# A gated-recurrence and linear-attention layer: column sums in another bank, sample gates in one accumulator, first values by halves

## The chip, the cores and the metric

The kernel runs on one core of one Trainium2 chip. Its time is the device time of that core in microseconds (us). Before the change it is 1463.81 us, the median of three runs (1462.57 to 1464.4). The core has five engines that run side by side, each through its own list of instructions in order: TensorE (PE) multiplies matrices, VectorE (DVE) and ScalarE (ACT) work on rows of elements, GpSimd (POOL) does some more of that, and SyncE (SP) mostly issues transfers (DMA). They wait for one another by semaphores.

## The reference

One layer works on a prompt of 2048 tokens and on 8 single-token samples, with a model width of 1024. Cut to what matters here:

```python
hn = _rmsnorm(x, g_norm) * (1.0 + scale[:, None]) + shift[:, None]
z = hn @ w_in
xa, za, q, k, v, glr, zg = jnp.split(z, SPLITS, axis=-1)
xc = conv_b + sum(xp[:, j:j + T] * conv_w[j] for j in range(CONV_W))
xb = xc.reshape(Bn, T, LRU_BLOCKS, LRU_BW)
gx = jax.nn.sigmoid(jnp.einsum('btnd,nde->btne', xb, w_gate_x).reshape(Bn, T, D_LRU) + b_gate_x)
ga = jax.nn.sigmoid(jnp.einsum('btnd,nde->btne', xb, w_gate_a).reshape(Bn, T, D_LRU) + b_gate_a)
log_a = (LRU_C * ga.astype(f32)) * jax.nn.log_sigmoid(lru_lambda.astype(f32))
a = jnp.exp(log_a)
u = jnp.sqrt(-jnp.expm1(2.0 * log_a)) * (gx * xc).astype(f32)
_, h = lax.associative_scan(_lin_comb, (a, u), axis=1)
y_lru = h.astype(x.dtype) * jax.nn.silu(za)
...
y_gla = o.reshape(Bn, T, D_GLA).astype(x.dtype) * jax.nn.silu(zg)
mix = jnp.concatenate([y_lru, y_gla], axis=-1) @ w_out
x = x + gate[:, None] * mix
```

Left out is the attention that makes o from q, k, v and the decay of glr. Both the prompt and the samples go through the layer, and the states (the last h, the last conv rows, the attention state) are outputs too.

## The kernel before

Products are made exact enough in float32 by splitting each operand into a high and a low part and adding three products (high by high, low by high, high by low): such triples are the lines L396 to L398, L1571, L1703 to L1706 and L1775 to L1777.

The prompt is worked in two halves of 1024 tokens. In the first half the columns of the input projection that are not attention come in **couples** (about 328 to 598 us): eight `Lru` couples (a block of 128 columns of xa and the same block of za) and three `Zg` couples (gate columns of the attention), in the order Lru 0 to 2, Zg(0, 3), Lru 3 to 7, Zg(0, 0), Zg(0, 1). Then come the attention heads, and in the second half (880 to 1115 us) eight Lru couples and three Zg couples again, then the output projection.

A couple computes a product of two 128-column blocks and two 512-token segments by seven products of 12 matmuls (`product`, q = 0 to 6, L1571), a scheme that saves an eighth of the matmuls by adding and subtracting operands first. Products 0 and 3 go to an accumulator x, 1, 4 and 6 to y, 2 and 5 to a third, zz. x and zz are PSUM banks of the tag `acc`, which has four of them; y is one of two `tp` banks. A third pair of banks, of the tags `kv` and `o`, is handed out in turn by `gps()` (L1473).

In an Lru couple the products' results go to ACT and DVE as they end. After product 3 and product 5 the convolution of a segment (`conv`: ACT L1682, L1683, DVE L1685 three times) gives `cv`; it is split into `xh` (ACT L1690) and `xl` (DVE L1691). The **gates** of a segment are then six matmuls into two `gps` banks (L1703, L1704, L1706), each read by an ACT tanh (L1707, into `tx` and `tg`). After the second segment follow on ACT exp (L1716), square root (L1717) and a table change (L1718, `one`), on DVE two products (L1724, L1725), the scan (L1731), and the multiplication of its result with the silu of za (`zs`, ACT L1135; DVE L1740), which is then stored to `mixd`. In a Zg couple the silu is multiplied with blocks of the attention output, which are loaded ahead (`load_o`); of the four blocks the third goes to the place `am`, the fourth to `xh` or `t2`.

For the samples, `combine` in the first half has PE form the column sums of the raw weights (`sample_cols`: eight matmuls L304 into a bank taken from `acc`, a copy to SBUF by ACT, L305, and after a delay of 1.25 units two small matmuls L310 into the same bank, which DVE L312 reads). The copy's place is `am`, a tile that else holds gate weights; in the first couple and in those that follow a Zg, whose third block of the attention output lies in `am`, it is a tile of the tag `xa`, the convolution's input. In the second half, `sample_gates` follows each Lru couple's second gates: three matmuls of 8 columns into a `gps` bank and a tanh, for each of two gates (L1775 to L1777, L1778).

`values` is the projection of one attention head's values: eight tiles of 128 tokens, each 24 matmuls over k = 0 to 7 (L396 to L398) into an `acc` bank; for the second half's first head it stands right behind the last couple. Its weights come in two transfers, k = 0 to 3 and k = 4 to 7 (SP, from `parts`).

The order of the work is that in which the code calls for it; pieces handed to `after(units, f)` are called when so many units have passed, and `behind(engine)` puts an instruction after the engine's last. A couple's `wait` (0.75) delays `combine`. The column sums of a couple are made two couples ahead of its own products. Within that, a scheduler settles the order of each engine.

Of the kernel before, what the change touches and what calls it, by code (L numbers as in the profile page):

```python
# [8 lines left out]
F32 = mybir.dt.float32  # L9
# [5 lines left out]
P = 128  # L15
D = 1024
KT = D // P
T = 2048
TH = T // 2
NS = 8  # L20
# [33 lines left out]
def hybrid_kernel(ctx, tc, i, o):  # L54
# [7 lines left out]
    def acc():  # L62
        return psum.tile([P, 512], F32, tag="acc", name="acc", bufs=4)
# [65 lines left out]
    hbx = cp.tile([P, KT], F32, name="hbx")  # L129
    hba = cp.tile([P, KT], F32, name="hba")  # L130
# [159 lines left out]
    zsam = cp.tile([P, 24, NS], F32, name="zsam")  # L290
# [102 lines left out]
    def value_mm(ps, c, w, n, kts):  # L393
        for kt in range(*kts):
            hi, lo, _ = w[kt // 4]
            PE.matmul(ps, part(0, kt, c), hi[:, kt % 4], start=kt == 0, stop=False)  # L396
            PE.matmul(ps, part(0, kt, c), lo[:, kt % 4], start=False, stop=False)  # L397
            PE.matmul(ps, part(1, kt, c), hi[:, kt % 4], start=False, stop=kt == KT - 1)  # L398
# [9 lines left out]
    begun = {}  # L408
# [501 lines left out]
    def values(half, h, w):  # L910
        first = h == HEADS[0]
        n = DV + (RANK if first else 0)
        vh, vl = new_values()
        turns = []
        for tt in range(8):
            c = slice(tt * P, (tt + 1) * P)
            ps = acc()
            value_mm(ps[:, :n], c, w, n, (0, KT))
            hi, lo = vh[tt // 4][:, tt % 4], vl[tt // 4][:, tt % 4]
            S.copy(hi, ps[:, :DV])  # L920
            V.tensor_tensor(lo, ps[:, :DV], hi.bitcast(F32), op=OP.subtract)
            if tt == 0 and half == 1 and first:
                raws = [raw_rows(V0 + h * DV, n, k0, 4) for k0 in (0, 4)]
            elif tt == 0:
                raws = [x[2] for x in w]
            if tt == 3 * half + 1 and own_samples(half, h):
                after(0.5, sample_values(h, raws, n))
            if len(turns) == 3 or tt == 7 and turns:
                turns.pop(0)()
            if first:  # L930
                turns.append(low_rank(ps[:, DV:n], slice(0, P), tt * P))
            tick(0.5)
        for f in turns:
            after(1, f, True)
        return vh, vl
# [535 lines left out]
    banks, turns = [0], [0, 0, 0, 1]  # L1471

    def gps():  # L1473
        banks[0] ^= 1
        return psum.tile([P, 512], F32, tag=("kv", "o")[banks[0]], name="gps", bufs=1)

    class Couple:
# [63 lines left out]
        def combine(self, q=G):  # L1541
            r = self.raw
            b11, b12, b21, b22 = [r[:, 4 * k:4 * k + 4, b] for k in range(2) for b in range(2)]
            if self.half == 0:
                tmp = am.rearrange("p c t -> p (c t)")
                if self.own_tmp:
                    tmp = lp.tile([P, 512 + 4], F32, tag="xa", name="tmp")
                sample_cols(lambda kt: r[:, kt].rearrange("p b n -> p (b n)"), 2 * P,
                            [(zsam[:, n], 1.0) for n in self.sam], tmp, acc, 1.25)
            t = self.t2 = lp.tile([P, 4, P], F32, tag="t2", name="t2")  # L1550
            q.tensor_tensor(b11, b12, b11, op=OP.subtract)
            q.tensor_tensor(t, b22, b11, op=OP.subtract)
            q.tensor_tensor(b12, b22, b12, op=OP.subtract)

        keep, wait, more, own_tmp = None, 0.75, (), False

        def begin(self):
            pass
# [42 lines left out]
    class Zg(Couple):  # L1601
# [8 lines left out]
                self.src = wtd[n]  # L1610

        def product(self, q):
            for n in {1: (0, 1), 2: (2,), 5: (3,)}.get(q, ()):
                if n == 3:
                    x = (lp.tile([P, 512], F32, tag="t2", name="o4") if self.turn == 1 else
                         lp.tile([P, 512], F32R, tag="xh", name="o4").bitcast(F32))
                elif n == 2 and self.turn == 1:
                    x = lp.tile([P, 512], F32R, tag="xl", name="o").bitcast(F32)
                else:
                    x = o_places[n]  # L1620
                self.o.append(x)
                self.load_o(n)
            super().product(q)
# [146 lines left out]

    def sample_gates(t):
        x, j = smp_lru, t.j
        for g, bias in enumerate((hbx, hba)):
            ps = gps()[:, :NS]
            PE.matmul(ps, t.wgh[:, g], x["h"][:, j], start=True, stop=False)  # L1775
            PE.matmul(ps, t.wgh[:, g], x["l"][:, j], start=False, stop=False)
            PE.matmul(ps, t.wgl[:, g], x["h"][:, j], start=False, stop=True)  # L1777
            S.activation((zsam[:, 16:24], x["t"])[g][:, j], ps, AF.Tanh, bias=bias[:, j:j + 1], scale=0.5)  # L1778
        x["n"] += 1
        if x["n"] == KT:  # L1780
            after(2, samples_lru)
# [58 lines left out]
    def couples(cs, lead=5, at={}):  # L1840

        n = len(cs)
        for k in (1, 2):
            cs[-k].turn = k
        for c, prev in zip(cs[1:], cs):
            c.own_tmp = isinstance(prev, Zg)
        cs[0].own_tmp = True
        uses = [(0, 0), (0, 1)]
        for m in range(n):
# [44 lines left out]
    w = None  # L1894
# [529 lines left out]
    for n in range(2, 16):  # L2424
        g = n - 1
# [88 lines left out]
```

## Time and profile before

| | us |
|---|---|
| median of 3 runs | 1463.81 |
| profiled execution | 1455.25 |
| its span | 1453.5 |
| PE busy | 1408.9 |
| DVE busy | 1063.0 |
| ACT busy | 726.3 |
| POOL busy | 206.7 |
| span of the first half's couples, about | 270 |
| span of the second half's couples, about | 235 |

One execution is profiled; its own time is 1455.25 us, below the median of the others. The views that the prediction quotes are the page (busy time of each engine), windows (busy time of PE, its weight loads PEld, DVE, ACT and POOL in a stretch, then the granted TensorE clock as a share of full speed, the DMA share and GB/s), the list of waits (which instruction stood still, behind which, total us, how often, longest), and the timeline (start, duration, engine, line, operation, output and inputs, count; in brackets the idle time before it and what ended it). A row of the timeline with x12 is twelve like instructions in a run.

### The profile page before, as it was taken

How to read it: one execution, taken by the hardware profiler on the slowest of the kernel's cores; microseconds unless marked ns; L12 is line 12 of the kernel's file. 1: busy time of each engine (PE TensorE's matmuls, PEld its weight loads, DVE VectorE, ACT ScalarE, POOL GpSimd, SP SyncE). 2: the span in 40 equal slices, each digit the busy share in tenths (PEclk: the TensorE clock that was granted, in tenths of full speed). 3: DMA queues.
4: the chain of work that ended last, by engine and by line, in shares of the span. 5: the costliest groups of instructions: out<-in, count | busy, mean ns of one | idle time of the engine just before them, and what ended most of it. 6: DMA issues, size and time to landing. Idle time of an engine off the chain costs nothing.

```text
span 1453.5 us, 22471 instructions
## 1 busy us (share of the span) xinstructions
PE 1408.9 (97%) x8113; PEld 1167.0 (80%) x8113; DVE 1063.0 (73%) x2357; ACT 726.3 (50%) x1343; POOL 206.7 (14%) x257
## 2 busy tenths in 40 slices
PE   7999999999999999899999999999999999999997
PEld 5888989886868777789898888787788787777886
DVE  5767976657869786666777864787855886588886
ACT  4634463635775877333343433767663622244332
POOL 0200154325223222001211100000012000000000
PEclk9999999999999999999999999999999999999999
DMA  9724666648678567964957528898879767684452
GB/s 327 268 87 157 255 218 216 236 139 299 248 243 288 178 228 254 341 222 150 342 176 242 188 100 308 277 303 284 275 239 384 310 242 263 235 331 145 143 168 102
DMA packets 173380, 341.89 MB, mean 235 GB/s; under 512 B 12466, under 2 KB 101842, under 8 KB 169677
## 3 DMA queue, kind: packets, MB, share of 16 engines
q1 hardware_dynamic: 136981, 275.82, 55.4%
q0 software_dynamic: 13680, 48.64, 8.7%
q10 hardware_dynamic: 22608, 15.99, 3.5%
q8 instruction: 64, 1.05, 0.3%
q14 instruction: 47, 0.39, 0.1%
HBM read 205.78 MB, written 134.69 MB: 234 GB/s over the span
## 4 chain that ended last, share of the span: by engine, by line
PE 65%; DVE 14%; DMA 7%; ACT 6%; issue 5%; POOL 2%; SPq 0%; ACTq 0%; POOLq 0%; DVEq 0%
PE acc L2161 11%; PE tp L2161 8%; PE acc L1571 8%; PE tp L1571 7%; PE acc L397 4%; PE acc L396 4%; PE acc L398 4%; PE acc L702 3%; PE acc L704 3%; PE acc L703 3%; DVE cv L1685 2%; PE po L1059 2%; DVE a L1731 1%; DVE op L1518 1%; DMA scratch<-in_x_prompt_dram 1%
## 5 line engine op out<-in xcount | busy, mean ns | idle before, releaser
L1571 PE MATMUL acc<-op,op 128*128 128x512 f32 x1056 | 257.3, 395 | 3.7 <-ACT zs L1135 3.7
L1571 PEld LDWEIGHTS acc<-op,op 128*128 128x128 f32 x1056 | 199.2, 190 | 48.4 <-ACT zs L1135 5.4
L1571 PE MATMUL tp<-op,op 128*128 128x512 f32 x792 | 195.2, 394 | 3.2 <-DVE acc L1581 1.8
L2161 PE MATMUL acc<-w,a 128*128 128x512 f32 (+1 forms) x792 | 187.7, 389 | 2.5 <-DVE w L2026 2.0
L2161 PEld LDWEIGHTS acc<-w,a 128*128 128x128 f32 x792 | 146.6, 188 | 39.1 <-issue 3.4
L1571 PEld LDWEIGHTS tp<-op,op 128*128 128x128 f32 x792 | 146.4, 188 | 38.5 <-issue 2.9
L396 PE MATMUL acc<-w,op 128*128 128x256 f32 (+1 forms) x508 | 150.8, 297 | 3.3 <-DMA w<-parts 2.0
L397 PE MATMUL acc<-w,op 128*128 128x256 f32 (+1 forms) x508 | 144.8, 285 | 0.4 <-DVE w L375 0.4
L398 PE MATMUL acc<-w,op 128*128 128x256 f32 (+1 forms) x508 | 144.9, 285 | 0.2 <-DVE op L271 0.2
L2161 PE MATMUL tp<-w,a 128*128 128x512 f32 x564 | 137.3, 393 | 0.0
L2161 PEld LDWEIGHTS tp<-w,a 128*128 128x128 f32 x564 | 105.1, 188 | 28.3 <-issue 5.2
L702 PE MATMUL acc<-op,w 128*128 128x512 f32 x296 | 121.1, 409 | 0.0
L704 PE MATMUL acc<-op,w 128*128 128x512 f32 x296 | 116.5, 394 | 0.0
L703 PE MATMUL acc<-op,w 128*128 128x512 f32 x296 | 115.9, 392 | 0.0
L396 PEld LDWEIGHTS acc<-w,op 128*128 128x128 f32 x508 | 97.0, 191 | 5.5 <-ACT op L1321 2.6
L397 PEld LDWEIGHTS acc<-w,op 128*128 128x128 f32 x508 | 96.3, 190 | 1.5 <-DVE w L375 0.6
L398 PEld LDWEIGHTS acc<-w,op 128*128 128x128 f32 x508 | 96.2, 189 | 0.9 <-DVE op L271 0.4
L2023 ACT CAST a<-s 128x512 fp32r<-128x512 f32 x61 | 36.5, 620 | 106.0 <-issue 35.6
L228 ACT ACTIVATE junk<-on 128x256 bf16<-128x256 f32 x64 | 26.8, 418 | 120.4 <-DVE on L1064 100.8
L1685 DVE SCALAR_TENSOR_TENSOR cv<-xa,vecT,cv 128x512 f32<-128x512 f32 x96 | 74.5, 776 | 6.7 <-ACT cv L1683 5.8
L1518 DVE TENSOR_TENSOR op<-raw,op 128x512 fp32r<-128x512 f32 x55 | 48.0, 876 | 39.3 <-ACT op L1517 39.3
L1060 DVE TENSOR_TENSOR states<-states,pkv 128x256 f32<-128x256 f32 x60 | 25.1, 418 | 59.3 <-PE po L1059 59.0
(444 smaller groups left out, 2802.8 us busy)
## 6 DMA issues: line engine op xcount, KB each, us to landing
wtd<-op SPq DMA_DIRECT2D x77, 512.0 KB
op<-wtd SPq DMA_DIRECT2D x77, 512.0 KB
w<-parts SPq DMA_DIRECT2D x16, 1024.0 KB
a<-mixd SPq DMA_DIRECT2D x63, 256.0 KB
parts<-w POOLq DMA_DIRECT2D x12, 1024.0 KB, 6.4
w<-wd SPq DMA_DIRECT2D x10, 1024.0 KB
wr<-in_w_in_dram SPq DMA_DIRECT2D x18, 512.0 KB
wada<-in_w_ada_dram SPq DMA_DIRECT2D x16, 512.0 KB
```

The costliest lines, as they stand in the source:

```text
L396: PE.matmul(ps, part(0, kt, c), hi[:, kt % 4], start=kt == 0, stop=False)
L397: PE.matmul(ps, part(0, kt, c), lo[:, kt % 4], start=False, stop=False)
L398: PE.matmul(ps, part(1, kt, c), hi[:, kt % 4], start=False, stop=kt == KT - 1)
L702: PE.matmul(ps[:, :n], hi[:, kt], a, start=kt == 0, stop=False)
L703: PE.matmul(ps[:, :n], hi[:, kt], b, start=False, stop=False)
L704: PE.matmul(ps[:, :n], lo[:, kt], a, start=False, stop=kt == KT - 1)
L1059: PE.matmul(po, qi[:, t], St[h], start=False, stop=True)
L1518: V.tensor_tensor(w[:, 1], x, w[:, 0].bitcast(F32), op=OP.subtract)
L1571: PE.matmul(ps, w[:, u, k], t[:, v, k], start=q < 3 and (k, u, v) == (0, 0, 0), stop=(k, u) == (3, 1), skip_group_check=True)
L1685: V.scalar_tensor_tensor(cv, xa[:, k:k + 512], cw[k], cv, op0=OP.mult, op1=OP.add)
L2023: S.copy(t[:, 0, k], (low(t) if src is None else src)[:, k])
L2161: PE.matmul(ps, t[:, u, k], w[:, v, k, c], start=(q < 3 or ps is own) and (k, u, v) == (0, 0, 0), stop=(k, u) == (3, 1), skip_group_check= ...
```

## The change

It has four parts. First, the column sums take a bank from `gps` in place of `acc`, their L310 comes after 1 unit in place of 1.25, and `wait` is 0.25 in place of 0.75. Second, the copy goes to `am` in every couple but the first; for this, the Zg couples of the first half other than the last load their third block one product later (q = 3 in place of 2), into a place of the tag `cv0`. Third, the sample gates of the second half use one `acc` bank: six matmuls first, then both tanhs. Fourth, in the second half's first head, the first three tiles of `values` run k = 0 to 3 before any of them runs k = 4 to 7.

```diff
@@ values
-        turns = []
+        turns, begun = [], []
+        if half == 1 and first:
+            for tt in range(3):
+                begun.append(acc())
+                value_mm(begun[tt][:, :n], slice(tt * P, (tt + 1) * P), w, n, (0, 4))
         for tt in range(8):
             c = slice(tt * P, (tt + 1) * P)
-            ps = acc()
-            value_mm(ps[:, :n], c, w, n, (0, KT))
+            ps = begun[tt] if tt < len(begun) else acc()
+            value_mm(ps[:, :n], c, w, n, (4 if tt < len(begun) else 0, KT))
@@ combine
-                            [(zsam[:, n], 1.0) for n in self.sam], tmp, acc, 1.25)
+                            [(zsam[:, n], 1.0) for n in self.sam], tmp, gps, 1)
...
-        keep, wait, more, own_tmp = None, 0.75, (), False
+        keep, wait, more, own_tmp = None, 0.25, (), False
@@ Zg.product
-            for n in {1: (0, 1), 2: (2,), 5: (3,)}.get(q, ()):
+            late = self.half == 0 and self.turn != 1
+            for n in {1: (0, 1), 2 + late: (2,), 5: (3,)}.get(q, ()):
...
+                elif n == 2 and late:
+                    x = lp.tile([P, 512], F32, tag="cv0", name="o")
@@ sample_gates
-        for g, bias in enumerate((hbx, hba)):
-            ps = gps()[:, :NS]
+        both = acc()
+        both = [both[:, g * NS:(g + 1) * NS] for g in range(2)]
+        for g, ps in enumerate(both):
             PE.matmul(ps, t.wgh[:, g], x["h"][:, j], start=True, stop=False)
             PE.matmul(ps, t.wgh[:, g], x["l"][:, j], start=False, stop=False)
             PE.matmul(ps, t.wgl[:, g], x["h"][:, j], start=False, stop=True)
+        for g, (ps, bias) in enumerate(zip(both, (hbx, hba))):
             S.activation((zsam[:, 16:24], x["t"])[g][:, j], ps, AF.Tanh, bias=bias[:, j:j + 1], scale=0.5)
@@ couples
-        for c, prev in zip(cs[1:], cs):
-            c.own_tmp = isinstance(prev, Zg)
         cs[0].own_tmp = True
```

Line numbers after the change are higher by 4 from L920 on, by 7 from about L1620 and by 8 from about L1775.

How this moves PE's instructions shows in a couple of the first half (the sixth Lru couple of that half). Before, from the column sums on (`acc_5497` is their bank, `xh_5387` the first segment's convolution):

```order
L304 MATMUL acc_5497<-raw_5327,fs_150 32x256 x8
L1571 MATMUL tp_5267<-op6_149,op_5391 128x512 x12
L1571 MATMUL acc_5544<-op2_1185,op_5416 128x512 x12
L1703 MATMUL gps_5564<-xh_5387,aml_125 128x512
L1704 MATMUL gps_5564<-xh_5387,aml_125 128x512
L1703 MATMUL gps_5567<-xh_5387,aml_125 128x512
L1704 MATMUL gps_5567<-xh_5387,aml_125 128x512
L1706 MATMUL gps_5564<-xl_5388,aml_125 128x512
L1706 MATMUL gps_5567<-xl_5388,aml_125 128x512
L1571 MATMUL acc_5401<-op3_147,op_5450 128x512 x12
L310 MATMUL acc_5497<-sel4_113,am_122 128x8 x2
```

After, from the same L304 on (its bank is `gps_5473`, the convolution's part `xh_5391`):

```order
L304 MATMUL gps_5473<-raw_5327,fs_150 32x256 x8
L1575 MATMUL tp_5493<-op1_1186,op_5353 128x512 x12
L1575 MATMUL tp_5281<-op6_149,op_5395 128x512 x12
L310 MATMUL gps_5473<-sel4_113,am_122 128x8 x2
L1575 MATMUL acc_5548<-op2_1185,op_5416 128x512 x12
L1710 MATMUL gps_5568<-xh_5391,aml_125 128x512
L1711 MATMUL gps_5568<-xh_5391,aml_125 128x512
L1713 MATMUL gps_5568<-xl_5392,aml_125 128x512
L1575 MATMUL acc_5401<-op3_147,op_5450 128x512 x12
L1575 MATMUL acc_5612<-op0_146,op_5470 128x512
L1710 MATMUL gps_5571<-xh_5391,aml_125 128x512
L1711 MATMUL gps_5571<-xh_5391,aml_125 128x512
```

L304 stands one product earlier, L310 before the third product in place of behind the fourth; the two gates of the first segment are apart, with 13 matmuls between them, and the second gate's bank `gps_5571` is the one that holds the column sums of `gps_5473`; its third matmul and the 11 other matmuls into `acc_5612` follow. Six of the eight Lru couples have this split.

On DVE, in the same couple, the reads of the column sums (L312) before, from the multiplication with the scan's result on:

```order
L1740 TENSOR_TENSOR zs_5256<-a_5352,zs_5256 128x512
L1740 TENSOR_TENSOR zs_5236<-a_5352,zs_5236 128x512
L1685 SCALAR_TENSOR_TENSOR cv_5525<-xa_5379,vecT_126,cv_5525 128x512
L1687 COPY xac_137<-xa_5379 128x3
L1581 TENSOR_TENSOR acc_5544<-tp_5479,p5_5557 128x512
L1685 SCALAR_TENSOR_TENSOR cv_5525<-xa_5379,vecT_126,cv_5525 128x512
L1709 SCALAR_TENSOR_TENSOR tx_5561<-tx_5561,cv_5381 128x512
L1674 MEMSET xa_5590 128x3
L1518 TENSOR_TENSOR op_5602<-t2_5295,op_5602 128x512
L1691 TENSOR_TENSOR xl1_5533<-cv_5525,xh1_5532 128x512
L312 TENSOR_SCALAR zsam_152<-acc_5497 128x8 x2
```

And after, where L1692 is the convolution (L1685 before) and L1747 the multiplication (L1740 before):

```order
L1739 COPY hc_138<-a_5356 128x1
L1747 TENSOR_TENSOR zs_5256<-a_5356,zs_5256 128x512
L1747 TENSOR_TENSOR zs_5236<-a_5356,zs_5236 128x512
L1692 SCALAR_TENSOR_TENSOR cv_5525<-xa_5383,vecT_126,cv_5525 128x512
L312 TENSOR_SCALAR zsam_152<-gps_5473 128x8
L1692 SCALAR_TENSOR_TENSOR cv_5525<-xa_5383,vecT_126,cv_5525 128x512
L312 TENSOR_SCALAR zsam_152<-gps_5473 128x8
L1585 TENSOR_TENSOR acc_5548<-tp_5493,p5_5561 128x512
```

The two reads moved ahead of the last part of the convolution, of the sum for the third product and of the split.

On PE at the start of the second half's first head, where `w_6273` holds k = 0 to 3 and `w_6275` k = 4 to 7, the last rows with the first weights and the first with the second, before:

```order
L396 MATMUL acc_6293<-w_6273,op0_6127 128x272
L397 MATMUL acc_6293<-w_6273,op0_6127 128x272
L398 MATMUL acc_6293<-w_6273,op0_6127 128x272
L396 MATMUL acc_6332<-w_6273,op0_6127 128x272
L397 MATMUL acc_6332<-w_6273,op0_6127 128x272
L398 MATMUL acc_6332<-w_6273,op0_6127 128x272
L396 MATMUL acc_6293<-w_6275,op3_6190 128x272
L397 MATMUL acc_6293<-w_6275,op3_6190 128x272
```

After:

```order
L396 MATMUL acc_6319<-w_6273,op0_6127 128x272
L397 MATMUL acc_6319<-w_6273,op0_6127 128x272
L398 MATMUL acc_6319<-w_6273,op0_6127 128x272
L396 MATMUL acc_6319<-w_6273,op0_6127 128x272
L397 MATMUL acc_6319<-w_6273,op0_6127 128x272
L398 MATMUL acc_6319<-w_6273,op0_6127 128x272
L396 MATMUL acc_6293<-w_6275,op3_6190 128x272
L397 MATMUL acc_6293<-w_6275,op3_6190 128x272
```

Behind the first tile's k = 0 to 3, one triple of `acc_6332` stood ahead of the second weights; now it is 24 matmuls, 12 each of the tiles `acc_6306` and `acc_6319`.

## The prediction, made before the changed kernel ran

> **What bounds the kernel now.** The page comes first: its header and its row for TensorE (PE).
>
> ```profile
> span 1453.5 us, 22471 instructions
> PE 1408.9 (97%) x8113; PEld 1167.0 (80%) x8113; DVE 1063.0 (73%) x2357; ACT 726.3 (50%) x1343; POOL 206.7 (14%) x257
> ```
>
> PE is busy for 97% of the span, so the matmuls set the time and everything that can be won without dropping matmuls lies in 1453.5 − 1408.9 = 44.6 us of PE idle, plus any time in which PE is busy at a lower clock. The change drops no matmul. The windows by stage say where that idle lies: span, PE busy, …, and PEclk, the granted clock, third from the end.
>
> ```profile
> 325.00:610.00 285.00, 271.61 (x1325) 213.99 (x1324) 219.37 (x321) 196.62 (x300) 78.11 (x61) 0.98 0.74 260
> 610.00:880.00 270.00, 269.06 (x1828) 238.43 (x1828) 189.53 (x651) 105.05 (x263) 30.67 (x43) 1.00 0.61 205
> 880.00:1110.00 230.00, 224.94 (x1003) 183.62 (x1002) 164.75 (x275) 152.78 (x234) 18.01 (x24) 1.00 0.87 291
> ```
>
> The first half's couples (325 to 610) have 13.4 us of idle, the GLA stage after them 0.9, the second half's couples (880 to 1110) 5.1. The GLA stage is so full that a gain ahead of it is carried through. PE's waits, by what ended them, in the list of waits (total, times, longest):
>
> ```profile
> PE acc L310 <- ACT tmp L305: 4.4, 2, 2.3
> PE acc L1571 <- ACT zs L1135: 3.7, 4, 1.3
> PE gps L1775 <- ACT tx L1707: 3.6, 4, 1.2
> PE acc L396 <- DMA w<-parts: 2.0, 2, 1.5
> ...
> PE gps L1703 <- ACT xh L1690: 1.4, 2, 0.9
> ```
>
> Four of these are what the change touches: 4.4 + 3.7 + 3.6 + 2.0 = 13.7 us. There is a hidden cost behind some of them. Windows laid around the two L310 stalls, the longest weights wait and one more stall (at 586.0) show the clock afterwards:
>
> ```profile
> 415.40:418.80 3.40, 1.10 (x8) 0.66 (x6) 3.40 (x7) 2.16 (x5) 0.00 (x0) 1.00 1.06 338
> 418.80:422.20 3.40, 3.40 (x10) 2.73 (x10) 2.59 (x8) 2.44 (x4) 1.60 (x1) 0.50 0.91 295
> 422.20:425.60 3.40, 3.40 (x16) 2.74 (x16) 1.52 (x3) 2.12 (x4) 1.67 (x1) 1.00 1.03 394
> 562.10:565.50 3.40, 1.34 (x9) 0.85 (x7) 3.40 (x7) 2.16 (x5) 0.00 (x0) 1.00 0.51 154
> 565.50:568.90 3.40, 3.40 (x10) 2.72 (x10) 3.01 (x7) 2.33 (x4) 1.60 (x1) 0.51 0.66 211
> 586.00:589.40 3.40, 1.80 (x8) 1.14 (x7) 3.40 (x7) 0.00 (x0) 0.00 (x0) 1.00 1.05 354
> 589.40:592.80 3.40, 3.17 (x14) 2.64 (x15) 0.98 (x3) 0.60 (x1) 0.00 (x0) 1.00 1.07 341
> 599.70:603.10 3.40, 1.84 (x13) 1.43 (x13) 1.88 (x3) 1.99 (x2) 0.00 (x0) 1.00 1.01 401
> 603.10:606.50 3.40, 3.40 (x17) 3.37 (x16) 1.44 (x5) 1.31 (x3) 0.00 (x0) 0.50 0.99 383
> ```
>
> A stretch in which PE was busy for 1.10, 1.34 or 1.84 of 3.40 us is followed by one at a granted clock of 0.5: 10 matmuls there, 16 in the next one. Half a clock for 3.4 us costs at most 1.7 us, and by these counts at least 3.4 × 6/16 = 1.3; I take **1.5** each. The stretch at 586.0 with 1.80 busy was not followed by one (1.00 from 589.4 on), so three of four such stalls had this cost.
>
> **The change part by part.**
>
> *Column sums (first half).* The two L310 stalls are of the sums of the two couples that follow a Zg, whose copy lay in the place `xa`.
>
> ```profile
> 417.90 0.37 ACT L305 COPY tmp<-acc 128x256 f32<-128x256 f32 x1 [0.28 <-DVE cv L1685]
> ```
>
> The copy L305 waited for the convolution on VectorE (DVE L1685) to be done with `xa`. With `am` as the place it does not: the 2.3 us stall and its twin go. −4.4, and the two slow stretches behind them −3.0. In every couple L304 comes one product of 12 matmuls earlier. Its rows must have landed by then; the list of waits, which goes down to 0.4 us, has no L304 behind a DMA, so I put nothing, at most 1 us at a Zg. The column subtractions on POOL (GpSimd) move ahead with it, and the third block that Zg loads on SP (SyncE) is issued one product later, into `cv0`; its reader is one couple step away. Both nothing; the dear case is a rival.
>
> The four zs stalls are the third product's accumulator waiting for a silu on ScalarE (ACT) to read the old one. Two couples keep two products each in the four `acc` banks, and the column sums were a fifth tenant; without them the bank was read long before: −3.7.
>
> In their place comes a **new wait**. The column sums now hold one of two `gps` banks until DVE's L312 has read it, and the second gate of the next couple wants that bank. Its PE time is counted from the end of the second segment's gates.
>
> ```profile
> 464.45 0.51 PE L310 MATMUL acc<-sel,am 128*128 128x8 f32 x4
> ...
> 468.60 0.62 PE L1706 MATMUL gps<-xl,aml 128*128 128x512 f32 x2
> 469.06 2.89 PE L1571 MATMUL tp<-op,op 128*128 128x512 f32 x12
> 471.79 2.88 PE L1571 MATMUL acc<-op,op 128*128 128x512 f32 x12
> ...
> 477.32 1.07 PE L304 MATMUL acc<-raw,fs 128*32 128x256 f32 x16
> 478.32 3.06 PE L1571 MATMUL tp<-op,op 128*128 128x512 f32 x12
> ```
>
> A product takes 471.79 − 469.06 = 2.73, L304 1.0, L310 0.5, three gate matmuls 3 × 2.73/12 = 0.7. By the new order six products, L304, L310, one gate and one matmul lie between: 16.4 + 1.0 + 0.5 + 0.7 + 0.2 = 18.8 us. The other side is a chain of ACT and DVE:
>
> ```profile
> 478.90 0.20 ACT L1718 ACTIVATE one<-a 128x1 f32<-128x1 f32 x1
> ```
>
> ```profile
> 479.14 1.41 DVE L1724 SCALAR_TENSOR_TENSOR a<-tg,a 128x1024 f32<-128x1024 f32 x1 [0.21 <-ACT one L1718]
> 480.58 2.20 DVE L1725 TENSOR_TENSOR tx<-tx,a 128x1024 f32<-128x1024 f32 x1
> 482.70 0.68 DVE L1518 TENSOR_TENSOR op<-raw,op 128x512 fp32r<-128x512 f32 x1
> 483.31 2.28 DVE L1731 TENSOR_TENSOR_SCAN a<-tg,tx 128x1024 f32<-128x1024 f32 x1
> ...
> 487.42 0.74 DVE L1685 SCALAR_TENSOR_TENSOR cv<-xa,vecT,cv 128x512 f32<-128x512 f32 x1
> ```
>
> DVE starts L1724 at 479.14 − 469.06 = 10.1 after the gates. The new order has L305 in the ACT chain in place of a cast (0.37 for 0.60), so 9.8. From 479.14 to the end of the second L1685, 488.16, are 9.0; one L1518 more (0.7) and the L312 bring it to 9.8. Sum 19.6 against 18.8, a wait of 0.8. L1725 takes 2.20 here for as many elements as L1724's 1.41; at 1.41 the wait is nothing. Between these I take 0.6, nearer to the row that is there, with 0 and 1.5 (one more L1518 in the way) as ends. Six couples have the split gates: **+3.6** (0 to +9). What is queued behind the waiting gate are 11 matmuls and the next segment's gates, so ACT's next tanh gets late with it and the next couple's chain starts later: it is a recurrence, and the wait comes back in each couple rather than growing. A wait of 0.6 slows no clock (the stretches above needed over 1.5 of idle).
>
> *First values of the second half.*
>
> ```profile
> 598.57 0.36 PE L396 MATMUL acc<-w,op 128*128 128x272 f32 x1 [0.48 <-DMA w<-parts]
> ...
> 600.41 0.29 PE L398 MATMUL acc<-w,op 128*128 128x272 f32 x1
> 602.25 0.36 PE L396 MATMUL acc<-w,op 128*128 128x272 f32 x1 [1.55 <-DMA w<-parts]
> ```
>
> PE did 15 matmuls before it needed the second weights, (600.41 − 598.57)/14 = 0.13 us each. With 24 more ahead (3.1 us) it reaches that point at about 603.8, after the 602.25 at which it went on. −1.55 and the third slow stretch, −1.5. The first wait (0.48) stays. Whether the copies and subtractions of this row hold up the third tile bounds it below: 0 to −3.1; I take −3.1, since they are issued as before and had ended by the time PE went on.
>
> *Sample gates (second half).* In four of eight couples PE waited between segment gates and sample gates for the tanh to empty a `gps` bank. With an `acc` bank of their own they don't: −3.6. But the next gates hang on ACT and DVE, not on PE: in two neighbouring couples PE already waits for xh, 1.4 in all. PE arriving earlier by 3.6 in four couples finds some of that: I give back 1.4, so **−2.2** (−3.6 to 0).
>
> **Sum** against the profiled execution (1455.25 around its span of 1453.5): −4.4 − 3.0 − 3.7 + 3.6 − 3.1 − 2.2 = −12.8. The slow stretches in it (4.5) are those of one execution; with three of four stalls followed by one, other executions have about 3.4 of the 4.5: −11.7. The median of the runs shown is 1463.81, 8.6 above the profiled one; I subtract the same 11.7 from it: **1452**.
>
> On the clock the Trainium skill speaks against me: "TensorE: Matmul & The Clock Gate", section "Why this matters for your kernels", has no drop below idle gaps of some 3 µs. By that rule stalls of 2.3, 2.1 and 1.55 would leave the clock alone, none of the 3.4 would be won, and the time would be that of rival 2. The trace disagrees where it shows 0.50 directly behind them.
>
> **The rivals.**
> 1. *Gates without the wait.* POOL lies elsewhere and the chain ends before PE: for it the 1.41 of L1724, against it the row of 2.20. −11.7 − 3.6 = −15.3: 1448.5.
> 2. *The slow stretches stay.* If they come at their own times and not from these stalls, −11.7 + 3.4 = −8.3: 1455.5. Three stalls with and one without speak for cause, not proof.
> 3. *The wait moves to `cv0`.* Zg's third block takes the place the next convolution writes; if it lands late, the L310 stalls return on that convolution with their slow stretches: −11.7 + 4.4 + ¾ × 3.0 = −5.0: 1459. For it: landing times of several us; against: it is read before the couple's last product.
> 4. *Slower: the second gate's bank comes late.* One mechanism, L312 behind the scan. It needs 1.9 us of waiting per couple, 1.3 more than worked out: then each wait is long enough for a slow stretch, (1.9 + ¾ × 1.5) × 6 = 18.2, more than the 15.3 of gains. At 2.1 it is 19.4, +4.1: 1468. For it: two ACT and three DVE instructions out of place are 1.3 us; against: in the couple shown DVE stood idle before 479.14 for what ACT makes, so only ACT's lag counts.
> 5. *Nothing moves*, 1464: other waits end at the same time in all four places.
>
> **How the numbers follow.** Forecast 0.48, rivals 0.14, 0.13, 0.12, 0.11 and 0.02. The forecast's own range, with the gate wait from 0 to 1.5 and sample gates from −3.6 to 0, is 1447 to 1460. The range 1446 to 1463 takes in rivals 1 to 3 and leaves out 4, 5 and a tail. About 0.2% (2.9 us) is what a measurement of this kernel can tell from no change. Faster by more: 0.45 of the forecast, rivals 1 and 2, 0.07 of rival 3: 0.79. Within: 0.03 + 0.05 + 0.02 = 0.10. Slower: 0.11.
>
> **What would show it.** In the list of waits of the changed kernel: no L310 behind L305 over 0.5, no third product behind the silu, no sample gate behind tanh, one weights wait of about 0.5, and instead a row of PE `gps` behind DVE's column sums with about six waits of 0.6 (0 for rival 1, over 1.9 for rival 4). The windows of 0.5 clock at these places would be gone, or rival 2 holds. A wait of ACT's convolution for SP's third block would be rival 3. I am wrong if the idle of 325 to 610 stays above 9 us, or if that of the second half's couples does not fall.

## The result, and the profile after

The changed kernel takes 1449.3 us (median of 6 runs, 1445.6 to 1450.5) beside 1460.6 us of the kernel before (6 runs, 1457.2 to 1464.4): a ratio of 0.9919, with a 95% interval of 0.9897 to 0.9941, or −8.6 to −15.0 us. The forecast was −11.7 us, to 1452. Timed a second time, on its own, it was 1449.1 beside 1460.2 (0.9922, 0.9899 to 0.9944).

The page and the list of PE's waits of the changed kernel (in the list: total us, times, longest):

```profile
span 1447.4 us, 22458 instructions
PE 1410.0 (97%) x8113; PEld 1168.9 (81%) x8113; DVE 1064.2 (74%) x2357; ACT 726.3 (50%) x1343; POOL 207.1 (14%) x257
```

```profile
PE gps L1710 <- DVE zsam L312: 5.8, 6, 2.2
PE gps L1710 <- ACT xh L1697: 2.8, 2, 1.7
PE tp L1575 <- DVE acc L1585: 2.3, 1, 2.3
...
PE acc L396 <- DMA w<-parts: 1.6, 1, 1.6
```

The three rows that the change aimed at are gone: L310 behind L305 (4.4), the third product behind the silu (3.7), the sample gates behind tanh (3.6). In their place stands the forecast's new row, a second gate that waits for DVE's L312, 6 times as forecast, but 5.8 us in place of 3.6. The xh row has grown from 1.4 to 2.8, which is just the 1.4 that the forecast gave back. L1585 (L1581 before) has grown from 1.8 to 2.3. Of the two weights waits there is one left, but of 1.6, not 0.48.

Where the time went by stage is read from windows cut at the same instruction in both kernels: the first gates of the first half, the first matmul of the second half's values, the last head's values, the first gates of the second half, the first matmul of the output projection. The four stretches from the first of these points to the last, in the kernel before (start and end, span, then PE busy and the other engines; the granted clock is third from the end):

```profile
363.47:598.57 235.10, 224.74 (x1066) 177.44 (x1064) 183.60 (x268) 169.18 (x256) 55.78 (x37) 0.99 0.71 247
598.57:793.72 195.15, 192.65 (x1374) 172.79 (x1375) 134.33 (x445) 76.92 (x191) 22.89 (x32) 0.99 0.71 238
793.72:902.21 108.49, 108.49 (x614) 93.45 (x613) 73.01 (x236) 41.38 (x92) 7.78 (x11) 1.00 0.55 188
902.21:1120.10 217.89, 212.83 (x949) 173.46 (x948) 158.86 (x268) 147.55 (x226) 20.27 (x27) 1.00 0.87 294
```

And after:

```profile
365.80:598.00 232.20, 222.48 (x1061) 175.76 (x1060) 182.76 (x266) 170.39 (x256) 56.19 (x37) 0.99 0.72 249
598.00:790.35 192.35, 190.74 (x1374) 170.97 (x1375) 132.97 (x444) 76.84 (x190) 22.92 (x32) 1.00 0.71 244
790.35:898.82 108.47, 108.47 (x614) 93.43 (x613) 73.22 (x237) 41.41 (x92) 7.79 (x11) 1.00 0.55 189
898.82:1113.20 214.38, 211.57 (x949) 173.82 (x948) 158.49 (x266) 146.37 (x226) 20.31 (x27) 1.00 0.89 300
```

The couples of the first half are 2.9 us shorter, the stretch with the first values 2.8, the second half's couples 3.5, and the stretch in which PE never waits is the same to 0.02 us: a gain ahead of it is indeed carried through. The profiled execution was 2.8 us late when the couples began (the first column sums, L304, at 330.03 in place of 327.24), in code that the change doesn't touch; by the first gates 0.5 of that was made up. The output projection at the end was 0.8 longer (1447.4 − 1113.2 beside 1453.5 − 1120.1), so that the spans differ by 6.1 and not by the 9.2 of the three stretches.

The rows also say how the 9.2 us came about. PE's idle time (span less busy time) fell by only 0.6, 0.9 and 2.3 us in the three stretches, 3.8 in all; the other 5.4 us are PE being busy for less time with the same matmuls (some records are missing, so the counts differ by a few). In the first half's couples, at which two of the four parts aim, 2.3 of the 2.9 us are of that second kind.

The waits are not all of it. Every run has its mean granted clock beside its span. Over 62 of the 63 runs of the kernel before in the experiments (the other took 3564 us and is left out) that was 0.9894 in the mean, over 12 runs of the changed kernel 0.9929. One minus that, times the span, is the clock that was not granted: 15.4 us before, 10.3 after. Among the 62 runs of the one kernel the time rises by 0.68 us for each such us (correlation 0.74), so by this estimate the 5.1 us less are worth about 3.5 us (0.68 × 5.1) of the 9.9 by which the means of these runs differ (1459.0 and 1449.1); 6.4 us are left for the waits. The slope is a fit to one kernel's runs, and nothing here shows that it holds between two kernels.

### The profile page after: what moved, and what is told of

Same layout as the page of the kernel before. It is cut to its first block, busy times and chain, and to the rows that moved or that the text cites. A ratio compares the mean times of both kernels' runs of the same rounds, so it can differ in the third digit from the quotient of the medians.

```text
span 1447.4 us, 22458 instructions
## 1 busy us (share of the span) xinstructions
PE 1410.0 (97%) x8113; PEld 1168.9 (81%) x8113; DVE 1064.2 (74%) x2357; ACT 726.3 (50%) x1343; POOL 207.1 (14%) x257
## 4 chain that ended last, share of the span: by engine, by line
PE 63%; DVE 15%; ACT 9%; DMA 8%; issue 3%; POOL 1%; SPq 1%; ACTq 0%; DVEq 0%; POOLq 0%
PE acc L2168 12%; PE tp L2168 8%; PE acc L1575 6%; PE tp L1575 5%; PE acc L702 4%; PE acc L704 4%; PE acc L703 3%; PE acc L397 3%; PE acc L396 3%; PE acc L398 3%; DMA mixd<-zs 2%; DVE cv L1692 2%; PE po L1063 2%; DVE op L1522 2%; DVE a L1738 2%
## 5 line engine op out<-in xcount | busy, mean ns | idle before, releaser
L1575 PE MATMUL tp<-op,op 128*128 128x512 f32 x792 | 190.3, 393 | 2.7 <-DVE acc L1585 2.3
L1692 DVE SCALAR_TENSOR_TENSOR cv<-xa,vecT,cv 128x512 f32<-128x512 f32 x96 | 76.4, 796 | 6.0 <-ACT cv L1690 5.3
L704 PEld LDWEIGHTS acc<-op,w 128*128 128x128 f32 x296 | 55.6, 188 | 12.6 <-DVE w L375 0.4
```

The source lines that it names most:

```text
L704: PE.matmul(ps[:, :n], lo[:, kt], a, start=False, stop=kt == KT - 1)
L1575: PE.matmul(ps, w[:, u, k], t[:, v, k], start=q < 3 and (k, u, v) == (0, 0, 0), stop=(k, u) == (3, 1), skip_group_check=True)
L1692: V.scalar_tensor_tensor(cv, xa[:, k:k + 512], cw[k], cv, op0=OP.mult, op1=OP.add)
```

## The experiments

All ratios are to the kernel before, timed beside the kernel of the row, with 95% intervals. One us is 0.07%.

| kernel | median us | before | ratio | interval |
|---|---|---|---|---|
| place of the copy alone (part 2) | 1455.6 | 1458.9 | 0.9977 | 0.9964 to 0.9989 |
| sums in `gps` and place (parts 1, 2) | 1455.5 | 1458.9 | 0.9982 | 0.9967 to 0.9997 |
| sample gates alone (part 3) | 1456.9 | 1458.9 | 0.9980 | 0.9964 to 0.9996 |
| first values alone (part 4) | 1454.3 | 1458.9 | 0.9980 | 0.9961 to 0.9999 |
| the whole change again | 1449.1 | 1460.2 | 0.9922 | 0.9899 to 0.9944 |
| whole, ACT reads the sums | 1448.6 | 1460.2 | 0.9914 | 0.9891 to 0.9937 |
| whole, sums' turn late | 1446.1 | 1460.2 | 0.9905 | 0.9884 to 0.9925 |
| whole without part 2 | 1449.7 | 1460.2 | 0.9931 | 0.9910 to 0.9953 |
| ACT reads, a Zg on POOL | 1449.2 | 1459.3 | 0.9939 | 0.9917 to 0.9960 |
| whole without part 4 | 1449.9 | 1459.3 | 0.9941 | 0.9919 to 0.9963 |
| whole without part 3 | 1451.7 | 1459.3 | 0.9951 | 0.9933 to 0.9969 |
| whole without parts 1 and 2 | 1451.7 | 1459.3 | 0.9947 | 0.9927 to 0.9967 |

### Each part alone

The place of the copy alone:

```diff
+            late = self.half == 0 and self.turn != 1
+            for n in {1: (0, 1), 2 + late: (2,), 5: (3,)}.get(q, ()):
...
+                elif n == 2 and late:
+                    x = lp.tile([P, 512], F32, tag="cv0", name="o")
...
-        for c, prev in zip(cs[1:], cs):
-            c.own_tmp = isinstance(prev, Zg)
```

> Only the place of the copied column sums is changed (am in every couple but the first, the third block of Zg in cv0); the sums stay in acc, late. If the two L310 stalls came from the place xa and the half-clock stretches from the stalls: L310 behind L305 falls from 4.4 to under 0.5, the 0.50 stretches at 419 and 566 are gone, the four zs waits (3.7) stay, time -4.4 to -7.4 (1453 to 1456 beside 1460.6). If the wait only moves (to cv0, or to the zs row): -2 at most. If the stretches come at their own times: the stalls go, the stretches stay, -4.4.

PE's waits of this kernel:

```profile
PE tp L1571 <- DVE acc L1581: 4.3, 2, 4.1
PE acc L1571 <- ACT zs L1135: 3.8, 5, 1.2
```

L310 behind L305 is gone from the list, so the place was its cause, and no wait for `cv0` came: rival 3 falls. The two half-clock stretches behind it are gone too. The time fell by 3.4 us (interval 1.6 to 5.2), less than the 4.4 to 7.4 expected. The wait for L1581, at the last Zg couples, has risen from 1.8 to 4.3, with a new half-clock stretch at it: 2.5 of the 4.4 us are waited for again there. DVE's timeline at that place (start, duration):

```profile
581.48 2.29 DVE L1734 TENSOR_TENSOR_SCAN a<-tg,tx 128x1024 f32<-128x1024 f32 x1
...
584.33 1.28 DVE L1743 TENSOR_TENSOR zs<-a,zs 128x512 f32<-128x512 f32 x2
585.52 0.69 DVE L1638 TENSOR_TENSOR zs<-zs,o 128x512 f32<-128x512 f32 x1
586.13 0.69 DVE L1581 TENSOR_TENSOR acc<-tp,p 128x512 f32<-128x512 f32 x1
```

The sum that PE needs (L1581) stands behind the last Lru couple's scan, its two multiplications and a product (L1638). A Zg couple has no gates, so PE is through it sooner than DVE is through that line. What PE gains before can be waited for here. That is a wait that the forecast did not price.

The other three parts alone were the edits of the change one by one.

> The column sums' bank, their earlier time and the copy's place are changed; the sample gates and the first values are as before. By the terms measured in the changed kernel: no L310 and no zs wait (-8.1), six waits of the second gate for DVE's L312 (+5.8), two slow stretches less and one more (-1.5): -3.8, 1456 to 1457 beside 1460.6, so no better than the place of the copy alone. If the sums' bank is worth its 3.7 as predicted and the new wait 3.6: -7.5. L1775 and the second weights' wait stay as before.

PE's waits:

```profile
PE gps L1706 <- DVE zsam L312: 7.3, 6, 2.2
PE gps L1778 <- ACT tx L1710: 3.1, 4, 0.9
PE acc L396 <- ACT op L1321: 2.6, 1, 2.6
```

The first reading held: the sums' bank with its new wait is worth no more than the place of the copy alone (0.9982 and 0.9977, the intervals overlap). −2.6 us (interval −0.4 to −4.8) also leaves out the −7.5 that the forecast's terms come to. The third row stands at k = 4 of the first values: here it is not the weights that are late but ACT's cast of the activations (L1321).

> Only the sample gates of the second half are in one acc bank. By the forecast: the L1775 row (3.6) is gone, xh waits rise from 1.4 to 2.8, net -2.2, 1458.4 beside 1460.6. By the landmarks of the changed kernel (902.2 to 1067.4 became 898.8 to 1060.8): -3.3. If the gates hang on ACT and DVE alone: 0. The first half is as before in its waits.

The L1775 row was gone and the xh row 2.6 (1.4 before); the ratio is −2.9 us, between the two figures expected, and zero is out by a little. In this kernel the first half is that of the kernel before, and yet PE waited 3.5 us for L1321 at k = 4 of the first values, where the profile before has 1.55 behind the weights. So what stands at that place differs between executions, and one profile doesn't price it.

> Only the first three tiles of the second half's first values run k 0 to 3 ahead of k 4 to 7. By the forecast: the second weights' wait (1.55) and the 0.50 stretch behind it go, the first wait (0.48) stays: -3.1, 1457.5 beside 1460.6. If the weights' transfers are late as a whole and the wait moves to the first: -1.5 or less. In the changed kernel the first wait was 1.6; if that comes from this part (not from the earlier end of the couples) it is 1.6 here too.

Here no wait for the weights is left at all, so the first wait of 1.6 in the changed kernel isn't this part's doing. Nor does it come in every execution: in the second profile of the changed kernel it was 0.2. At k = 4 two smaller waits have come, for ACT and DVE:

```profile
603.48 0.39 PE L396 MATMUL acc<-w,op 128*128 128x272 f32 x1 [0.69 <-ACT op L1325]
...
604.74 0.39 PE L398 MATMUL acc<-w,op 128*128 128x272 f32 x1 [0.74 <-DVE op L1326]
```

The forecast's lower bound for this part, that the copies and subtractions hold it up, was not idle: 1.4 of 1.55 came back in this execution, and the 3.4 us behind 605.8 ran at a clock of 0.52. In the timed runs the part was worth −2.9 us all the same (interval −0.1 to −5.7).

### One part left out

> The changed kernel without its fourth part (first values tile by tile as before). If the parts add: 1449.1 + 2.9 = 1452.0, ratio to before 0.994 to 0.995. If the earlier end of the couples makes this part worth more, because operands and weights of k 4 to 7 are then later beside PE: a wait of 2 to 4 at that place and 1453 to 1454.

> The changed kernel without its third part (sample gates in two gps banks as before). L1775-like waits of 3.2 to 3.6 are back. If the part is worth what it is alone: +2.9, 1452.0. By the landmarks +3.3. If ACT and DVE set the second half's couples: 0.

> The changed kernel without its first and second part (column sums in acc, late, copy in xa behind a Zg). L310 4.4 and zs 3.7 are back, the gate wait for L312 is gone. If the parts add by what they are alone: +2.6 to +3.3, 1452. If the forecast's terms hold (-4.4 -3.7 +5.8 and two slow stretches less): +4 to +5, 1453 to 1454. The whole was 0.992 of before and the three alone come to 0.994 together, so one of the three has to be worth more in company: the run in which more than 2.9 is lost names it.

The three edits are those above, left out of the whole (`no_values` is the whole without part 4, `no_gates` without part 3, `no_sums` without parts 1 and 2). The waits came back as expected: two for the weights, 2.5 us in all; the sample gates behind tanh, 3.2; L310 4.4 and the third product behind the silu 3.7, without L312. Ratios of 0.9941, 0.9951 and 0.9947 are 0.2 to 0.3% above the whole (0.992), and the three alone were 0.2% each. Each does about a third, as far as intervals of 0.2% to either side can tell. Alone they multiply to 0.9982 × 0.9980 × 0.9980 = 0.9942, which is at the upper end of the whole's two intervals; whether they gain in company can't be told from these runs, and all three runs lost about 3 us or more, so they name no one part that does.

The last part left out was the place of the copy, with the sums in `gps`:

```diff
-            late = self.half == 0 and self.turn != 1
-            for n in {1: (0, 1), 2 + late: (2,), 5: (3,)}.get(q, ()):
+            for n in {1: (0, 1), 2: (2,), 5: (3,)}.get(q, ()):
...
+        for c, prev in zip(cs[1:], cs):
+            c.own_tmp = isinstance(prev, Zg)
```

> The changed kernel without its second part: the copy of the sums of the couples that follow a Zg goes to xa, and Zg's third block to am at q = 2. If xa is what held L310 up: two L310 or gate waits of about 2 us come back with their slow stretches, +4 to +7 against the changed kernel. If the bank was what mattered: 0.

L310 behind L305 came back (4.1 in 2), as the first reading says, but the row of L312 fell from 5.8 in 6 waits to 4.3 in 4, and the median is 0.6 us above the whole. In two couples an L310 stall stands where the gate wait stood, and the time hardly moved; 4 us more, the low end of the first reading, are just inside the interval. No half-clock stretch followed these two stalls of 1.6 and 2.5 us in the profile.

### The new wait, taken away and moved

ACT reads the sums in place of DVE:

```diff
             for a, (d, scale) in enumerate(dst):
-                V.tensor_scalar(d, po[:, a * NS:(a + 1) * NS], scale, None, op0=OP.mult)
+                if bank is gps:
+                    S.copy(d, po[:, a * NS:(a + 1) * NS])
+                else:
+                    V.tensor_scalar(d, po[:, a * NS:(a + 1) * NS], scale, None, op0=OP.mult)
```

> The changed kernel, with the first half's column sums read out of their gps bank by ACT (two copies of 128x8) in place of DVE's L312, which stood behind the scan. If the new wait is DVE's place in line: the row gps behind L312 (5.8) goes, no gate wait takes its place, the slow stretch at 539 goes: -5.8 to -7.3 against the changed kernel, 1442 to 1444 beside 1449.3. If the couple's length is set by the whole chain of ACT and DVE anyway: the waits come back at the gates as waits for xh or tanh, 0 to -2. ACT gives 22 small copies of about 0.2 us.

PE's waits:

```profile
PE tp L1578 <- DVE acc L1588: 5.9, 2, 5.1
PE gps L1713 <- ACT xh L1700: 3.6, 4, 1.1
```

The row of L312 is gone, and the gates of a segment stand together again; so its cause was DVE's place in line. The list also says where the gain went: 5.1 us in one wait at the last Zg couples, the place seen above, and from 582.3 to 589.1, in the wait and behind it, two stretches of 3.4 us at half clock. From the first gates to the first values it took 231.9 us, as in the whole change (232.2). The profiled span is 1442.5, but the median is only 0.5 us below the whole change: the wait went as the first reading says, the time as the second, for a third reason.

The sums' small matmuls later:

```diff
-                            [(zsam[:, n], 1.0) for n in self.sam], tmp, gps, 1)
+                            [(zsam[:, n], 1.0) for n in self.sam], tmp, gps, 1.25)
```

> The changed kernel with the small matmuls L310 after 1.25 units as before, so DVE reads the sums one sum and one split later, and the scheduler puts the second gate three matmuls later. The wait for L312 grows from 1.0 to about 1.9 each (6 times, 11.4 in all). If waits of that size bring half-clock stretches, +5.6 and several stretches of 1.5: +8 to +12 against the changed kernel, 1457 to 1461, the price of rival 4. If the stretches have another cause: +5.6, and the mean granted clock stays.

This was a miss on both readings: 1446.1, faster than the whole (0.9905 beside 0.9922, though the intervals overlap), and the row of `gps` behind L312 has 5.0 us in 8 waits of at most 0.9. DVE's timeline around 530 us, where the whole change has its longest gate wait, shows why the wait there is short. The whole change:

```profile
528.58 1.23 DVE L1731 SCALAR_TENSOR_TENSOR a<-tg,a 128x1024 f32<-128x1024 f32 x1 [1.35 <-ACT one L1725]
530.06 0.69 DVE L1522 TENSOR_TENSOR op<-raw,op 128x512 fp32r<-128x512 f32 x1 [0.25 <-ACT op L1521]
530.67 1.22 DVE L1732 TENSOR_TENSOR tx<-tx,a 128x1024 f32<-128x1024 f32 x1
531.80 0.16 DVE L1694 COPY xac<-xa 128x3 f32<-128x3 f32 x1
531.87 0.68 DVE L1522 TENSOR_TENSOR op<-raw,op 128x512 fp32r<-128x512 f32 x1
532.47 2.28 DVE L1738 TENSOR_TENSOR_SCAN a<-tg,tx 128x1024 f32<-128x1024 f32 x1
```

With the later turn:

```profile
526.57 1.23 DVE L1731 SCALAR_TENSOR_TENSOR a<-tg,a 128x1024 f32<-128x1024 f32 x1 [0.47 <-ACT one L1725]
527.83 1.22 DVE L1732 TENSOR_TENSOR tx<-tx,a 128x1024 f32<-128x1024 f32 x1
528.98 0.68 DVE L1522 TENSOR_TENSOR op<-raw,op 128x512 fp32r<-128x512 f32 x1
529.58 2.28 DVE L1738 TENSOR_TENSOR_SCAN a<-tg,tx 128x1024 f32<-128x1024 f32 x1
```

I had moved L312 in my mind and left the rest of DVE's line as it was. The second gate did stand three matmuls later on PE, but the scheduler also put one operand subtraction (L1522) fewer ahead of the scan, which starts 3.0 us behind L1731 in place of 3.9. Because the waits stayed small, the price of rival 4 was not tested.

The scheduler moved one thing more, at the last Zg couples. The sum that PE waits for there stands directly behind the scan:

```profile
579.57 2.28 DVE L1738 TENSOR_TENSOR_SCAN a<-tg,tx 128x1024 f32<-128x1024 f32 x1
581.77 0.67 DVE L1585 TENSOR_TENSOR acc<-tp,p 128x512 f32<-128x512 f32 x1
```

In the whole change five other instructions stand between the two, and the sum starts at 587.18, 2.4 us behind the scan's end. PE's wait for L1585 is 1.0 here in place of 2.3, and from the first gates to the first values it took 228.4 us, the least of all the profiles. So that wait is a matter of the sum's place in DVE's line; no run here moved the sum alone.

### The place where it is given back

```diff
-            V.tensor_tensor(z, z, self.o[((0, 0), (1, 1), (0, 1), (1, 0)).index((s, dt))], op=OP.mult)
+            (G if self.half == 0 and self.turn == 2 else V).tensor_tensor(z, z, self.o[((0, 0), (1, 1), (0, 1), (1, 0)).index((s, dt))], op=OP.mult)
```

> The kernel in which ACT reads the sums, and in which the second-last Zg couple of the first half has its products with the attention output on POOL in place of DVE. There the gain of the couples was lost again: PE waited 5.1 us for a sum that stood in DVE's line behind the scan and those products. If DVE's line is the bound at that place: three products of 0.6 us less ahead of it, the wait falls from 5.1 to about 3.3, one slow stretch of two goes, -2 to -4 against the version before (1445 to 1446). If POOL slows DVE while both work, or the scan itself is what is late: 0 to +1.

The wait for L1588 rose, from 5.1 to 6.6. DVE with the products on its own line (the kernel in which ACT reads the sums):

```profile
576.69 1.22 DVE L1735 TENSOR_TENSOR tx<-tx,a 128x1024 f32<-128x1024 f32 x1
...
578.42 2.29 DVE L1741 TENSOR_TENSOR_SCAN a<-tg,tx 128x1024 f32<-128x1024 f32 x1
580.62 0.67 DVE L1525 TENSOR_TENSOR op<-t,op 128x512 fp32r<-128x512 f32 x1
...
581.27 1.28 DVE L1750 TENSOR_TENSOR zs<-a,zs 128x512 f32<-128x512 f32 x2
```

With the products on POOL, first DVE, then POOL:

```profile
576.38 2.20 DVE L1735 TENSOR_TENSOR tx<-tx,a 128x1024 f32<-128x1024 f32 x1
578.50 1.75 DVE L1525 TENSOR_TENSOR op<-t,op 128x512 fp32r<-128x512 f32 x1
580.17 2.28 DVE L1741 TENSOR_TENSOR_SCAN a<-tg,tx 128x1024 f32<-128x1024 f32 x1
...
582.56 2.10 DVE L1750 TENSOR_TENSOR zs<-a,zs 128x512 f32<-128x512 f32 x2
```

```profile
575.67 1.83 POOL L1645 TENSOR_TENSOR zs<-zs,gls 128x512 f32<-128x512 f32 x1 [4.24 <-ACT zs L1142]
577.47 2.23 POOL L1645 TENSOR_TENSOR zs<-zs,o 128x512 f32<-128x512 f32 x1
580.82 2.69 POOL L1645 TENSOR_TENSOR zs<-zs,o 128x512 f32<-128x512 f32 x1 [1.12 <-ACT zs L1142]
```

Three products of 0.6 us left DVE's line, and three DVE operations that started while POOL was at a product became slower by 1.0, 1.1 and 0.8 us: 2.9 lost for 1.8 won. Each ended about its own time after POOL's product did: 1.08 us (578.58 − 577.50) for 1.22, 0.55 for 0.67, 1.15 for 1.28, as if it had waited for POOL to be done. The Trainium skill says so beforehand: "GPSIMD Engine Reference", section "Specifications", has GpSimd share its SBUF interfaces with VectorE, with contention for VectorE's instructions of two SBUF inputs. The rows agree for the tensor products. The scan, which reads two inputs too, took 2.28 as without; but it had started 0.65 us ahead of POOL's third product, and that product is the longest of the three, 2.69. So the row doesn't show that a scan is spared.

## Why the prediction was right

The time came out as forecast, and the waits that went and the one that came did so by the mechanisms it gave. The sizes of its parts did not come out, and the total is in part luck: by the stretches, the first half's couples gave 2.9 us for 7.5 forecast, the first values 2.8 for 3.1, the second half's couples 3.5 for 2.2.

- **PE bounds, and a gain ahead of the full stage is carried**: shown, by 108.49 and 108.47 us for the stretch without waits.
- **L310 and zs, −8.1 us of waits**: the rows are gone, and L310 went with the place alone. The gain that was added up from them is not there: −4.4 − 3.0 − 3.7 + 3.6 = −7.5, and alone these two parts gave −2.6 (−0.4 to −4.8). The forecast had set a sign for being wrong, an idle time above 9 us from 325 to 610, and by that sign it was wrong here: 285.00 − 274.76 = 10.2 (9.8 in the second profile).

```profile
325.00:610.00 285.00, 274.76 (x1371) 217.39 (x1370) 222.56 (x323) 199.89 (x304) 78.96 (x62) 0.99 0.75 262
```

  By its terms it should have been 13.4 − 4.4 − 3.7 + 3.6 − 1.55 = 7.4. On the other side stand 2.2 us more of the new wait, 1.1 of the weights' first wait and 0.5 at the last Zg couples, which is 3.8 for the 2.8 that are missing. The other sign, the idle time of the second half's couples, did fall, from 5.1 to 2.8.
- **The new wait, +3.6**: the mechanism was right, in six couples and behind L312, and it went when ACT read the sums. The size was off: 5.8. Of the six single waits five were 0.60 to 0.87, near the 0.8 to 0.6 worked out, and one 2.2. In that couple L1731 stood 1.35 us for ACT (its row stands above, at 528.58), because ACT's xh had waited 1.21 us for the convolution:

```profile
521.23 0.62 ACT L1697 CAST xh<-cv 128x512 fp32r<-128x512 f32 x1 [1.21 <-DVE cv L1692]
```

  In the second profile two couples had 2.2 and the row was 7.4. The step took one couple's chain for all of them. They differ by what else falls into the chain: the 2.20 of L1725 in the prediction, against 1.22 of the same operation at 530.67 above, had started while POOL was at a subtraction (L1553, 479.54 to 481.70), and ended 1.08 us after it, like the three operations in the last experiment.
- **First values, −3.1**: the second weights' wait went, alone −2.9 us. But the wait ahead of it grew from 0.48 to 1.6 in the profiled execution (0.2 in the second), and at k = 4 the operands' casts are next. The term of the waits was 0.4 (2.0 to 1.6) rather than 1.55 there; the stretch from the first values on, which holds only the second of the two waits, is shorter by 2.8 with the half-clock stretch that went.
- **Sample gates, −2.2**: −3.6 + 1.4 by the rows, as worked out, and PE's idle time there fell by 2.3. The stretch is 3.5 shorter; the other 1.3 are PE's busy time.
- **What was not priced**: L1585 at the last Zg couples, +0.5 here, 5.1 in one wait where ACT reads the sums, and 1.0 in all where the sum stands directly behind the scan.
- **The clock, −3.4**: by the runs' own clocks 5.1 us less were not granted, worth 3.5 at the slope of 0.68. The sum of the waits alone is −4.4 − 3.7 + 5.8 − 0.4 − 2.2 + 0.5 = −4.4, where the forecast had −8.3. So the total was right with a wait sum that was too good by 3.9 us; the runs leave 6.4 us for what the clock does not explain, and 2.0 us of that are not accounted for.

That the half-clock stretches come from stalls (against rival 2) is borne out, with a correction. Of the 33 such stretches between 35 and 1430 us in the 14 profiles of this study (some of them two on end), 32 began in a stall of PE of about 1.2 us or more or within 2.5 us of its end, and the other one behind the two stalls of 0.7 seen above, a size that the forecast had held to slow no clock. But not every stall has one. Windows of the changed kernel around its two longest stalls:

```profile
535.20:538.60 3.40, 1.17 (x5) 0.70 (x5) 3.40 (x9) 0.79 (x2) 0.00 (x0) 1.00 1.01 250
538.60:542.00 3.40, 3.40 (x10) 2.60 (x10) 3.39 (x7) 3.23 (x6) 1.15 (x1) 0.59 0.90 309
585.50:588.90 3.40, 1.05 (x5) 0.85 (x5) 2.37 (x4) 0.00 (x0) 0.00 (x0) 1.00 1.06 383
588.90:592.30 3.40, 3.40 (x16) 2.79 (x16) 0.96 (x2) 0.60 (x1) 0.00 (x0) 1.00 1.06 356
```

The 2.23 us stall is followed by half clock, the 2.35 us one is not. Over the same profiles, counting PE's single stalls between 35 and 1430 us and whether the granted clock fell below 0.6 within 4.5 us of their end:

| stall, us | times | followed by half clock |
|---|---|---|
| 1.2 to 1.5 | 11 | 1 |
| 1.5 to 2.0 | 28 | 10 |
| 2.0 to 2.5 | 22 | 12 |
| above 2.5 | 6 | 6 |

Just below the first row, at 1.17 to 1.19 us, lie 17 more, of which 3 were followed. The forecast's three of four was too high for stalls of 1.5 to 2.5 us: it is 22 of 50. The rule that the prediction weighed from the Trainium skill ("TensorE: Matmul & The Clock Gate", section "Why this matters for your kernels"), with no drop below some 3 µs of idle, does not hold here: 23 of the 61 stalls of 1.2 to 2.5 us were followed by one. A stall at the same place with the same length is followed by half clock in one execution and not in another. Since each execution shows only a few of them, a comparison of two profiles (−6.1 us here) says less than the timed runs (−11.3 between medians).

## What to carry to other kernels

When a wait of the bound engine is removed, look for the next place at which the other engines' line ends late, and price that too: here the sum behind the last scan took back up to 5 us of what the couples gained, and 1.0 where it stood directly behind the scan. A bank that is lent to something else comes free when the last reader's engine gets to it in its line, so look what stands ahead of the reader there. Moving the reader to ScalarE took the wait away, but only 0.5 us of the time. And a stall of 1.5 to 2.5 us on TensorE costs more than itself: as an estimate from this kernel, add 22/50 of the 1.5 us of a stretch at half clock, 0.7 us in the mean, before comparing edits. Last, when a sign of being wrong has been set, read it even if the total came out right.

## What was not expected of the hardware

- Half clock after a stall comes in some executions and not in others below 2.5 us (22 of 50 for 1.5 to 2.5, 6 of 6 above). The spread of one kernel's runs goes with the mean granted clock: 1451.8 to 1465.3 us among 62 runs of the kernel before, at clocks between 0.994 and 0.985 (correlation 0.74, so about half of the variance).
- A VectorE operation of 128x512 took 0.67 us alone and 1.75 when it started while POOL was at a product, one of 128x1024 1.22 and 2.20: about its own time from the end of POOL's product on.
